# Expert layer on one core: forty-four finished activation tiles instead of thirty, gate chunks of sixteen tokens, gate builds placed between products

## The chip, the cores and the metric

One core of one Trainium2 chip. The metric is the device time of one execution in microseconds (us), here the median of three runs. PE is the matrix engine, PEld its weight load, DVE the vector engine, ACT the scalar engine, POOL GpSimd, SP the engine that issues most DMAs (SPq its queue).

## What is computed

512 tokens of width 1024 pass two transformer blocks. The change touches only the expert layer ("PEER") of the first. Each token picks 128 of 16384 experts (8 heads, 16 each); an expert is a row of `peer_u` and a row of `peer_v`:

```
u = peer_u[ix]                                   # 128 rows of 1024 for each token
a = gelu(einsum('td,thkd->thk', hx, u))
out = einsum('thk,thkd->td', gates * a, peer_v[ix])
```

The kernel computes this densely for the first 384 tokens (all 16384 activations, times a gate matrix that is zero where an expert was not picked) and by gathered rows for the last 128 tokens.

## The kernel before

All large products are float32 split into a high and a low part: `split` (L96, L97) writes `whi` on ACT and `wlo` on DVE or POOL, and three matmuls take the place of one. Weights come in loads of 1 MB (`wraw`, two buffers), each split in two halves (`whi`, `wlo`, four buffers).

The expert layer, `peer`, runs in this order:

1. **Heads.** Eight times: query product, scores, top-k on DVE (`head`), and between them a *group*: `u_group(g)` multiplies 256 experts with 384 tokens (48 matmuls of 384 columns, tile `lin`, lines L126 to L128) and ACT applies Gelu into two activation tiles `ga` (L521). Groups 0 to 6 lie here, 7 to 9 behind the last head. Then ACT takes the Exp of the gate scores `gt` (L657), DVE normalizes.
2. **Preparation and builds.** `prep` transposes expert numbers and gates (`ps_tr`, `tr`). Then 96 *builds* (`g_build`), each for four tokens: DVE makes two one-hot tiles `o1`, `o2` (L700, L701, six buffers each), POOL multiplies one by the gates (L702), PE multiplies them (`ps_g`, L704, four matmuls in the program, eight instructions in the trace), ACT copies the result into a staging tile `stg` (L706). Every 32 tokens (eight builds) the 2 MB of `stg` are written to DRAM (`gd`; the last chunk is `gl`, in three pieces). Groups 10 to 14 lie among the builds. Fifteen groups are thirty finished tiles `ga`, the 2 * U1 of the code.
3. **Tiles.** 128 times `v_tile(e)`: load 128 experts of `peer_v`, split them, multiply `ga` by the gates of four tiles' fetch `gq` (DVE, L792), split that into `gah` (ACT) and `gal` (DVE, L97), and 18 matmuls of 512 columns into six accumulators (`acc`, L801). The first of them needs `gah`, the fifth `gal`. From tile 21 on every second tile is followed by one more group (15 to 63), whose tiles go to a ring of RING = 10 buffers.
4. **Gathers** for the last 128 tokens run beside the tiles: POOL issues a gather of 128 rows (L740, 256 in all), DVE takes it with a dot product (L753) or a scaled add (L751). Four row buffers, eight from tile 30 on. A gather issued behind tile e waits for the end of tile e - 2 (PACE = 2). One is taken for each of the first 20 tiles, then nine for each four tiles.

Each engine works through a list of its own in order, and what stands behind a waiting instruction of its list waits too. A scheduler makes the lists from the order of the code and its own estimate of when things are ready.

## Time and profile before

| | |
|---|---|
| median of 3 runs | 2979.46 us (2977.13 to 2981.54) |
| the profiled execution | 2983.46 us, span of the trace 2981.7 us |
| busy share PE / PEld / DVE / ACT / POOL | 96% / 82% / 67% / 41% / 24% |
| chain that ended last, by engine | PE 72%, DVE 11%, DMA 7%, issue 5%, ACT 3%, POOL 2% |
| from the last head's scores to the last tile | 383.5 to 1548.3 us of the span |

Matmuls are pipelined, so that a PE shown as busy is not always one that does a new matmul as soon as it could. What a stretch could take at best is therefore read from the distance at which equal blocks of matmuls follow each other, and not from busy time.

### The profile page before, as it was taken

Reading aid. Unit: us, or ns where it says so; the run is one execution under the profiler, and the core shown is the slowest. Engines: PE = TensorE matmul, PEld = TensorE weight load, DVE = VectorE, ACT = ScalarE, POOL = GpSimd, SP = SyncE. Lnnn points to the kernel's source line nnn. Section 1 sums busy time; section 2 is a strip of 40 time slices with the busy share of each in tenths; the row PEclk is TensorE's granted clock in tenths of the full one; section 3 lists DMA queues with packets and bytes.
Section 4 is the critical chain, followed back from the end, with each engine's and each line's share of the span. In section 5 each row is a group of like instructions: output and inputs, shape, how many; then the busy total and the mean of one; then the engine's idle time right before and its main releaser. Section 6 shows DMA issues by size and latency. Waiting matters only on the chain.

```text
span 2981.7 us, 39362 instructions
## 1 busy us (share of the span) xinstructions
PE 2865.8 (96%) x14925; PEld 2442.2 (82%) x14925; DVE 1994.3 (67%) x3922; ACT 1220.4 (41%) x2017; POOL 724.0 (24%) x551
## 2 busy tenths in 40 slices
PE   7989988699999999999999999999999999999998
PEld 5778988678999998999976767888878888878886
DVE  7879988777877767787775455444557766654453
ACT  6543347633333333333344344223345555433223
POOL 0013458525554554455410000000021100100000
PEclk9999999899999999999999999999999999999999
DMA  7552234687987888788752222222221111122221
GB/s 258 181 198 86 86 113 199 253 282 280 353 312 280 287 297 293 277 297 295 290 178 77 71 71 76 94 99 99 99 75 55 44 42 36 50 99 99 99 99 57
DMA packets 133022, 487.19 MB, mean 163 GB/s; under 512 B 10593, under 2 KB 60129, under 8 KB 96610
## 3 DMA queue, kind: packets, MB, share of 16 engines
q1 hardware_dynamic: 95104, 349.33, 33.3%
q0 software_dynamic: 36864, 134.23, 12.1%
q8 instruction: 117, 1.92, 0.3%
q10 hardware_dynamic: 866, 1.13, 0.1%
q14 instruction: 71, 0.58, 0.1%
HBM read 455.29 MB, written 29.36 MB: 163 GB/s over the span
## 4 chain that ended last, share of the span: by engine, by line
PE 72%; DVE 11%; DMA 7%; issue 5%; ACT 3%; POOL 2%; SPq 0%; POOLq 0%; DVEq 0%; ACTq 0%
PE lin L126 15%; PE lin L127 15%; PE lin L128 15%; PE acc L801 10%; DMA rows<-peer_v,Ei 3%; PE ps_g L704 2%; DMA rows<-peer_u,Ei 1%; DVE wlo L97 1%; PE ps_x L1295 1%; PE psc L948 1%; PE ps_y L1301 1%; PE po L971 1%; POOL wlo L97 1%; PE in L260 1%; ACT whi L96 1%
## 5 line engine op out<-in xcount | busy, mean ns | idle before, releaser
L96 ACT ACTIVATE whi<-wraw 128x1024 fp32r<-128x1024 f32 (+2 forms) x500 | 522.1, 1045 | 1046.2 <-PE lin L127 678.0
L126 PE MATMUL lin<-xah,whi 128*128 128x512 f32 (+1 forms) x2112 | 782.8, 371 | 18.4 <-ACT ga L521 10.0
L128 PE MATMUL lin<-xah,wlo 128*128 128x512 f32 (+1 forms) x2112 | 777.9, 368 | 2.6 <-POOL wlo L97 2.6
L127 PE MATMUL lin<-xal,whi 128*128 128x512 f32 (+1 forms) x2112 | 778.5, 369 | 0.0
L97 DVE TENSOR_TENSOR wlo<-wraw,whi 128x1024 fp32r<-128x1024 f32 (+2 forms) x388 | 477.2, 1231 | 185.9 <-ACT whi L96 179.3
L97 POOL TENSOR_TENSOR wlo<-wraw,whi 128x1024 fp32r<-128x1024 f32 x112 | 289.7, 2600 | 834.8 <-ACT whi L96 660.8
L126 PEld LDWEIGHTS lin<-xah,whi 128*128 128x128 f32 x2112 | 399.1, 189 | 69.5 <-ACT ga L521 10.6
L128 PEld LDWEIGHTS lin<-xah,wlo 128*128 128x128 f32 x2112 | 399.2, 189 | 45.6 <-POOL wlo L97 3.0
L127 PEld LDWEIGHTS lin<-xal,whi 128*128 128x128 f32 x2112 | 399.3, 189 | 43.6 <-issue 2.4
L753 DVE CUSTOM_DVE_ANT_0 rows<-rows,hrow 128x1024 f32<-128x1024 f32 x128 | 184.2, 1439 | 118.6 <-DMA rows<-peer_u,Ei 118.5
L801 PE MATMUL acc<-whi,gah 128*128 128x512 f32 x768 | 239.6, 393 | 22.9 <-ACT gah L96 22.9
L751 DVE SCALAR_TENSOR_TENSOR gacc<-rows,acol,gacc 128x1024 f32<-128x1024 f32 x128 | 191.2, 1494 | 92.1 <-DMA rows<-peer_v,Ei 91.7
L801 PE MATMUL acc<-whi,gal 128*128 128x512 f32 x768 | 239.3, 393 | 7.5 <-DVE gal L97 7.5
L801 PE MATMUL acc<-wlo,gah 128*128 128x512 f32 x768 | 239.4, 393 | 4.0 <-DVE wlo L97 4.0
L740 POOL DMA_INDIRECT rows<-peer_u,Ei x128 | 156.0, 1218 | 202.3 <-PE acc L801 146.1
L127 PE MATMUL lin<-hl,whi 128*128 128x512 f32 x512 | 200.1, 391 | 0.0
L126 PE MATMUL lin<-hh,whi 128*128 128x512 f32 x512 | 199.3, 389 | 0.0
L128 PE MATMUL lin<-hh,wlo 128*128 128x512 f32 x512 | 199.2, 389 | 0.0
L740 POOL DMA_INDIRECT rows<-peer_v,Ei x128 | 157.5, 1230 | 166.6 <-PE acc L801 132.0
L801 PEld LDWEIGHTS acc<-whi,gah 128*128 128x128 f32 x768 | 144.5, 189 | 50.4 <-ACT gah L96 23.1
L801 PEld LDWEIGHTS acc<-whi,gal 128*128 128x128 f32 x768 | 144.9, 189 | 40.2 <-DVE gal L97 9.5
L801 PEld LDWEIGHTS acc<-wlo,gah 128*128 128x128 f32 x768 | 145.1, 189 | 37.2 <-DVE wlo L97 6.2
(460 smaller groups left out, 4163.3 us busy)
## 6 DMA issues: line engine op xcount, KB each, us to landing
wraw<-peer_ut SPq DMA_DIRECT2D x64, 1024.0 KB
wraw<-peer_v SPq DMA_DIRECT2D x64, 1024.0 KB
wraw<-w_up SPq DMA_DIRECT2D x32, 1024.0 KB
wraw<-w_down SPq DMA_DIRECT2D x32, 1024.0 KB
gd<-stg SPq DMA_DIRECT2D x11, 2048.0 KB
gq<-gd SPq DMA_DIRECT2D x32, 704.0 KB
ada_w<-w_ada SPq DMA_DIRECT2D x20, 1024.0 KB
wraw<-dn_w_in SPq DMA_DIRECT2D x16, 1024.0 KB
```

Source lines behind the costliest of these rows:

```text
L96: self.nc.scalar.activation(hi, x, AF.Copy)
L97: ins = (eng or self.nc.vector).tensor_tensor(lo, x, hi.bitcast(F32), op=ALU.subtract)
L126: nc.tensor.matmul(ps[:, :n], hi[:, i], xh[:, k, :n], start=(i == 0), stop=False)
L127: nc.tensor.matmul(ps[:, :n], hi[:, i], xl[:, k, :n], start=False, stop=False)
L128: nc.tensor.matmul(ps[:, :n], lo[:, i], xh[:, k, :n], start=False, stop=(k == ks[1] - 1))
L260: nc.tensor.matmul(acc[f], w[:, f * P:(f + 1) * P], v[:, k, :], start=(k == 0 and n == 0), stop=(k == NK - 1 and n == 2))
L704: nc.tensor.matmul(ps[:, t, :], o1[:, t, :], o2[:, t, :], start=True, stop=True)
L740: dma = nc.gpsimd.indirect_dma_start(out=rows[n], out_offset=None, in_=io[src], in_offset=bass.IndirectOffsetOnAxis(ap=Ei[:, j:j + 1], axi ...
L751: nc.vector.scalar_tensor_tensor(gacc, t, w, gacc, op0=ALU.mult, op1=ALU.add)
L753: nc.vector.tensor_tensor_reduce(t, t, hrow, 1.0, 0.0, op0=ALU.mult, op1=ALU.add, accum_out=w)
L801: mm = nc.tensor.matmul(acc[t][d], w[:, ts], r[:, d * T:(d + 1) * T], start=(e == 0 and f == 0), stop=(e == P - 1 and f == 2))
L948: nc.tensor.matmul(psc[u][:, :w], qT[us, j, qs], kT[us, j, :w], start=True, stop=True)
```

## The change

- `U1` 15 to 14, `RING` 10 to 16: 28 tiles in the first pool, 16 in the ring, which is now opened ahead of the builds. `last = (28 + 16) / 2 = 22` groups are finished ahead of the first tile, 44 tiles.
- Group 10 moves ahead of the preparation, and the Exp waits for the Gelu of group 9 (`held`).
- `GQ` 32 to 16: a chunk is four builds, 1 MB; 24 chunks. `GE = 8`: one fetch `gq` serves eight tiles (1.5 MB) in place of four (0.75 MB); runs of 512 bytes as before.
- `tick`: in groups 11 to 18, six builds are placed between the eight steps of each product. Groups 12 and 16 split on DVE, the others of them on POOL.
- `gate`: the first matmul of group 11 stands behind the preparation's transposes, and groups 19 to 21 behind the last build.
- Row buffers: `ROWS` 3 in place of 4, `MORE` 6 in place of 4: three, then nine from tile 28 on. Gathers taken: one for each of tiles 0 to 27, five for each two tiles from 28 to 111, one to tile 120, then two.
- The groups between tiles are 22 to 63, after tiles 29, 31, ..., 111.

```
-U1 = 15
-RING = 10
-MORE = 4
+U1 = 14
+RING = 16
+ROWS = 3
+MORE = 6
...
-                    nc.tensor.matmul(ps[:, :n], hi[:, i], xh[:, k, :n], start=(i == 0), stop=False)
+                    mm = nc.tensor.matmul(ps[:, :n], hi[:, i], xh[:, k, :n], start=(i == 0), stop=False)
+                    if self.gate is not None:
+                        self.after(mm, self.gate)
+                        self.gate = None
...
+                    if self.tick is not None:
+                        self.tick(k)
...
-                for g in range(7, 10):
+                for g in range(7, 11):
                     u_group(g, nc.gpsimd)
+                    if g == 9:
+                        held = box["gelu"]
...
-                nc.scalar.activation(g3, g3, AF.Exp)
+                self.after(nc.scalar.activation(g3, g3, AF.Exp), held)
...
-            GQ = 32
+            GQ = 16
+            GE = 8
...
+            ah.append(st.enter_context(tc.tile_pool(name="p_ah1", bufs=RING)))
...
-                            nc.tensor.transpose(ps[:, t, :], src[:, t, :], self.ident)
+                            self.gate = nc.tensor.transpose(ps[:, t, :], src[:, t, :], self.ident)
...
-                for g in range(10, U1):
-                    u_group(g, nc.gpsimd)
-                    pull(len(todo) if g > 12 else 32)
+                last = (2 * U1 + RING) // 2
+                self.tick = lambda k: pull(k % 4 != 2)
+                for g in range(11, last - 3):
+                    u_group(g, (nc.gpsimd, None)[g % 4 == 0])
+                self.tick = None
                 pull(len(todo))
+                self.gate = box["g"]
+                for g in range(last - 3, last):
+                    u_group(g)
...
-                    i = n % (4 + MORE) if len(pools) > 1 else n % 4
-                    pool, bufs = (sp, 4) if i < 4 else (pools[1], MORE)
+                    i = n % (ROWS + MORE) if len(pools) > 1 else n % ROWS
+                    pool, bufs = (sp, ROWS) if i < ROWS else (pools[1], MORE)
...
-                    if e % 4 == 0:
-                        g = sp.tile([P, NQ, 4, GQ], F32, tag="gq", name="gq")
-                        nc.sync.dma_start(out=g[:, :NQ - 1], in_=gd[:, :, e:e + 4, :].rearrange("q p e t -> p q e t"))
+                    if e % GE == 0:
+                        g = sp.tile([P, NQ, GE, GQ], F32, tag="gq", name="gq")
+                        nc.sync.dma_start(out=g[:, :NQ - 1], in_=gd[:, :, e:e + GE, :].rearrange("q p e t -> p q e t"))
...
-                    gather(1 if e < 2 * RING else 2 + (e % 4 == 0))
+                    gather(2 + (e % 2 == 0) if 2 * U1 <= e < P - RING else 1 + (e > P - 8))
                     n = e + RING
-                    if n >= 2 * U1 and n % 2 == 1 and n < P:
+                    if n >= 2 * U1 + RING and n % 2 == 1 and n < P:
                         u_group(n // 2, (None, nc.gpsimd)[n // 2 % 2])
```

Three places show how the lists move (names with numbers are buffers; the two kernels' lines differ by a few).

ACT behind the last head's scores; `ga` is a Gelu, `gt` the Exp. Before:

```order
L96 ACTIVATE whi_3804<-wraw_3802 128x1024
L521 ACTIVATE ga_3705<-lin_3680 128x384
L96 ACTIVATE whi_3835<-wraw_3802 128x1024
L521 ACTIVATE ga_3736<-lin_3711 128x384
L657 ACT_TABLE_LOAD
L657 ACTIVATE gt_1865<-gt_1865 128x512
L521 ACT_TABLE_LOAD
L521 ACTIVATE ga_3769<-lin_3744 128x384
```

The same place now (the Gelus `ga_3769` to `ga_3833` lie ahead of these rows):

```order
L99 ACTIVATE whi_3963<-wraw_3930 128x1024
L531 ACTIVATE ga_3864<-lin_3839 128x384
L99 ACTIVATE whi_4042<-wraw_4040 128x1024
L531 ACTIVATE ga_3897<-lin_3872 128x384
L99 ACTIVATE whi_4142<-wraw_4040 128x1024
L531 ACTIVATE ga_3928<-lin_3903 128x384
L669 ACT_TABLE_LOAD
L669 ACTIVATE gt_1865<-gt_1865 128x512
L99 ACTIVATE whi_4244<-wraw_4242 128x1024
L531 ACT_TABLE_LOAD
L531 ACTIVATE ga_3961<-lin_3936 128x384
```

The Exp stood ahead of the Gelus of groups 7 to 9 (`ga_3769` to `ga_3928`) and stands behind them now.

PE in the middle of the builds; each `ps_g` row is one build. Before:

```order
L704 MATMUL ps_g<-o_4196,o_4195 128x128 x4
L126 MATMUL lin<-xah,whi 128x384
L127 MATMUL lin<-xal,whi 128x384
L704 MATMUL ps_g<-o_4207,o_4206 128x128 x4
L128 MATMUL lin<-xah,wlo 128x384
L126 MATMUL lin<-xah,whi 128x384
L704 MATMUL ps_g<-o_4220,o_4219 128x128 x4
```

Now, in the same stretch:

```order
L716 MATMUL ps_g<-o_4213,o_4212 128x128 x4
L129 MATMUL lin<-xah,whi 128x384
L133 MATMUL lin<-xal,whi 128x384
L134 MATMUL lin<-xah,wlo 128x384
L129 MATMUL lin<-xah,whi 128x384
L133 MATMUL lin<-xal,whi 128x384
L134 MATMUL lin<-xah,wlo 128x384
L716 MATMUL ps_g<-o_4230,o_4229 128x128 x4
L129 MATMUL lin<-xah,whi 128x384
L133 MATMUL lin<-xal,whi 128x384
L134 MATMUL lin<-xah,wlo 128x384
L716 MATMUL ps_g<-o_4255,o_4254 128x128 x4
```

Two or three matmuls of a group stood between two builds; three or six do now, four on average.

ACT around the last build (`stg` copies builds, `gah` belongs to the first tile). Before:

```order
L706 ACTIVATE stg_5155<-ps_g_5222 128x4x128
L706 ACTIVATE stg_5155<-ps_g_5233 128x4x128
L96 ACTIVATE gah_5406<-ga_2307 128x384
L96 ACTIVATE gah_5442<-ga_2338 128x384
L96 ACTIVATE gah_5474<-ga_2540 128x384
```

Now:

```order
L718 ACTIVATE stg_5596<-ps_g_5642 128x4x128
L99 ACTIVATE whi_5788<-wraw_5786 128x1024
L531 ACTIVATE ga_5689<-lin_5664 128x384
L99 ACTIVATE whi_5819<-wraw_5786 128x1024
L531 ACTIVATE ga_5720<-lin_5695 128x384
L99 ACTIVATE whi_5873<-wraw_5871 128x1024
L531 ACTIVATE ga_5753<-lin_5728 128x384
L99 ACTIVATE gah_5878<-ga_2307 128x384
L99 ACTIVATE gah_5912<-ga_2338 128x384
L99 ACTIVATE whi_5907<-wraw_5871 128x1024
L531 ACTIVATE ga_5784<-lin_5759 128x384
```

The first `gah` followed the last copy at once; now three Gelus of the held groups lie between (19 twice, then the first of 20), and the second Gelu of group 20 (`ga_5784`) lies behind the first two `gah`.

## Rows read from the trace of the kernel before

**Rows 1.** Windows by stage: length, busy (count) of five engines, PE clock, DMA share, GB/s.
```profile
383.50:438.30 54.80, 44.80 (x249) 44.12 (x248) 41.78 (x139) 18.47 (x27) 27.30 (x14) 0.91 0.29 96
438.30:571.00 132.70, 122.76 (x961) 120.94 (x960) 116.81 (x184) 108.97 (x113) 106.88 (x98) 0.99 0.49 199
571.00:594.00 23.00, 0.06 (x2) 0.04 (x1) 5.13 (x9) 2.58 (x5) 4.88 (x5) 0.56 0.91 319
594.00:694.00 100.00, 94.29 (x396) 76.50 (x397) 73.49 (x112) 32.46 (x45) 26.59 (x25) 0.96 0.83 281
694.00:1502.00 808.00, 803.96 (x4081) 732.67 (x4080) 614.00 (x678) 282.37 (x395) 416.93 (x274) 1.00 0.82 296
1502.00:1548.30 46.30, 43.08 (x182) 34.80 (x180) 29.71 (x32) 16.14 (x23) 5.00 (x4) 0.96 0.55 197
```

**Rows 2.** Chain that ended last: start, length, what; two blocks of two tiles.
```profile
702.51 8.20 PE acc L801 x36
719.05 8.20 PE acc L801 x36
```

**Rows 3.** Waits of PE, whole span: us in total, times, longest.
```profile
PE acc L801 <- ACT gah L96: 22.9, 1, 22.9
PE lin L126 <- ACT ga L521: 10.0, 2, 8.9
PE ps_g L704 <- POOL o L702: 9.9, 5, 2.4
PE acc L801 <- DVE wlo L97: 4.0, 5, 1.1
```

**Rows 4.** Timeline behind the last head: start, length, engine, what, [idle before <-releaser].
```profile
406.31 0.63 ACT L657 ACTIVATE gt<-gt 128x512 f32<-128x512 f32 x1 [12.09 <-DVE gt L636]
408.79 0.69 PE L126 MATMUL lin<-xah,whi 128*128 128x384 f32 x1 [8.91 <-ACT ga L521]
```

**Rows 5.** Groups of lines, 450 to 565 us (busy, mean ns, idle before); then POOL's timeline.
```profile
L706 ACT ACTIVATE stg<-ps_g 128x512 f32<-128x512 f32 x80 | 86.2, 1094 | 23.2 <-PE ps_g L704 17.2 <-issue 2.8
L702 POOL TENSOR_TENSOR o<-o,tr 128x512 f32<-128x512 f32 x82 | 83.6, 1045 | 9.1 <-DVE o L701 5.9 <-PE ps_g L704 2.6 <-PE lin L128 0.6
L97 POOL TENSOR_TENSOR wlo<-wraw,whi 128x1024 fp32r<-128x1024 f32 x4 | 9.5, 2377 | 13.3 <-ACT whi L96 13.3
...
443.33 14.08 POOL L702 TENSOR_TENSOR o<-o,tr 128x512 f32<-128x512 f32 x14
```

**Rows 6.** Timeline from the last builds to the first tile, five engines.
```profile
566.39 4.63 PE L704 MATMUL ps_g<-o,o 128*128 128x128 f32 x40
572.99 1.29 SPq L712 DMA_DIRECT2D gl<-stg  x3
581.43 1.13 POOL L740 DMA_INDIRECT rows<-peer_u,Ei  x1 [13.29 <-DMA gl<-stg]
589.74 1.23 DVE L753 CUSTOM_DVE_ANT_0 rows<-rows,hrow 128x1024 f32<-128x1024 f32 x1 [7.97 <-DMA rows<-peer_u,Ei]
592.67 1.49 DVE L792 TENSOR_TENSOR ga<-ga,gq 128x384 f32<-128x384 f32 x3
593.38 0.94 ACT L96 ACTIVATE gah<-ga 128x384 fp32r<-128x384 f32 x2 [20.42 <-DVE ga L792]
```

**Rows 7.** Timeline of two gathers: issue on POOL, take on DVE, and a fetch between.
```profile
600.34 1.01 POOL L740 DMA_INDIRECT rows<-peer_u,Ei  x1 [8.16 <-PE acc L801]
605.50 1.22 DVE L753 CUSTOM_DVE_ANT_0 rows<-rows,hrow 128x1024 f32<-128x1024 f32 x1 [1.48 <-DMA rows<-peer_u,Ei]
608.50 1.11 POOL L740 DMA_INDIRECT rows<-peer_u,Ei  x1 [3.14 <-DVE wlo L97]
608.83 0.37 SPq L783 DMA_DIRECT2D gq<-gd  x1
618.97 1.23 DVE L753 CUSTOM_DVE_ANT_0 rows<-rows,hrow 128x1024 f32<-128x1024 f32 x1 [5.54 <-DMA rows<-peer_u,Ei]
```

**Rows 8.** Timeline of PE among the last ten tiles.
```profile
1521.38 0.73 PE L801 MATMUL acc<-whi,gal 128*128 128x512 f32 x2 [1.79 <-DVE gal L97]
```

More of the change, by code (lines that the diff above doesn't have):

```diff
@@ L516, in peer @@
             xd = dram.tile([P, NK, T], F32, name="xd")
+            box = {}
             def u_group(g, eng=None):
@@ L520, in gelu @@
                     A[e] = ah[e >= 2 * U1].tile([P, NG], F32, tag="ga", name="ga")
-                    nc.scalar.activation(A[e], ps[:, :NG], AF.Gelu)
+                    box["gelu"] = nc.scalar.activation(A[e], ps[:, :NG], AF.Gelu)
                 self.linear(io["peer_ut"], xh, xl, gelu, chunks=[g], n=NG, eng=eng)
@@ L703, in g_build @@
                     for t in range(4):
-                        nc.tensor.matmul(ps[:, t, :], o1[:, t, :], o2[:, t, :], start=True, stop=True)
+                        box["g"] = nc.tensor.matmul(ps[:, t, :], o1[:, t, :], o2[:, t, :], start=True, stop=True)
                     q = t0 % GQ
@@ L727, in peer @@
                        for t in range(3)]
-                rows = {-1: sp.tile([P, D], F32, tag="rows", bufs=4, name="rows")}
+                rows = {-1: sp.tile([P, D], F32, tag="rows", bufs=ROWS, name="rows")}
                 gacc = sp.tile([P, D], F32, bufs=1, name="gacc")
@@ L780, in v_tile @@
                 def v_tile(e):
-                    if e % 4 == 0:
-                        g = sp.tile([P, NQ, 4, GQ], F32, tag="gq", name="gq")
-                        nc.sync.dma_start(out=g[:, :NQ - 1], in_=gd[:, :, e:e + 4, :].rearrange("q p e t -> p q e t"))
+                    if e % GE == 0:
+                        g = sp.tile([P, NQ, GE, GQ], F32, tag="gq", name="gq")
+                        nc.sync.dma_start(out=g[:, :NQ - 1], in_=gd[:, :, e:e + GE, :].rearrange("q p e t -> p q e t"))
                         a, b, last = [v for v in gl if v[0] <= e < v[1]][0]
-                        nc.sync.dma_start(out=g[:, NQ - 1], in_=last[:, e - a:e - a + 4, :])
+                        nc.sync.dma_start(out=g[:, NQ - 1], in_=last[:, e - a:e - a + GE, :])
                         gq["g"] = g
@@ L824, in peer @@
                 for t in (2, 1, 0):
-                    o = sp.tile([P, D], F32, tag="rows", bufs=4, name="orow")
+                    o = sp.tile([P, D], F32, tag="rows", bufs=ROWS, name="orow")
                     for d in range(2):
```

8 lines of the change are left out of this document (4 added, 4 removed).

## The prediction, made before the change was run

> **What bounds the kernel now.** First the stages from the last head's scores to the last tile [rows 1]: 1164.8 us in which PE is shown busy nearly all the time except between the builds and the first tile. Busy time doesn't tell what PE could do at best, so the second view is the chain that ended last [rows 2]: two blocks of 36 tile matmuls begin 16.54 us apart, one lasts 8.20 us, and the 48 matmuls of a group fill the other 8.34 us. So a tile matmul costs 0.228 us (a tile of 18: 4.10 us) and a group matmul 0.174 us. Forty build instructions in a row take 4.63 us [rows 6], 0.116 us each, 0.93 us for a build of eight. With these prices the bare work of each stage, and what it loses, are:
>
> - Stage 1, 383.5 to 438.3: 237 group matmuls (45 of group 6, groups 7 to 9 and the first behind the preparation) 41.2 us, nine transposes at 0.116 us 1.0 us. Lost: 12.6 us.
> - Stage 2, to 571.0: 192 group matmuls 33.4 us, 96 builds 88.9 us. Lost: 10.4 us.
> - Stage 3, to 594.0: no work at all. Lost: 23.0 us.
> - Stage 4, to 694.0: 22 tiles, 90.2 us. Lost: 9.8 us.
> - Stage 5, to 1502.0: 49 groups and 96 tiles, 802.4 us. Lost: 5.6 us.
> - Stage 6, to 1548.3: 10 tiles, 41.0 us. Lost: 5.3 us.
>
> PE is the bound, and 66.7 us are lost on it. Third, PE's own waits [rows 3] say to whom: one wait of 22.9 us for the first `gah`, 10.0 us for Gelus, 9.9 us for POOL's part of the builds, 4.0 us for weight splits among the tiles. The rest is mostly the clock: its mean is 0.91, 0.96 and 0.96 in stages 1, 4 and 6 [rows 1], so 8% of stage 4, 8 us, ran at 1.2 in place of 2.4 GHz and lost 4 us, after PE had stood still.
>
> The change neither adds nor removes a matmul: groups 15 to 21 move from between the tiles to a place ahead of them. So the sum is: which of the lost microseconds go, and which come.
>
> **The Exp (stage 1).** Before, the Exp stood ahead of the Gelus of group 7 and waited 12.09 us for DVE's last scores, until 406.31; PE, whose two product buffers were full, waited 8.91 us until 408.79 [rows 4] and then ran slow. Now the Gelus of groups 7 to 9 come first. PE ends group 9 at 383.5 + 189 x 0.174 = 416.3, ten us behind the time at which the Exp's input is ready, and group 10, 8.3 us, runs on PE while ACT and DVE finish the gates. All 12.6 us go. What is late next is the first build: its transposes are followed by copies on ACT, two compares on DVE and a multiplication on POOL, for which 48 matmuls were cover and now only 18 are, 3.1 us. I put 1 us of waiting there (bounds 0 and 3), counted in stage 2.
>
> **The builds (stage 2).** The work is now 384 group matmuls, 66.7 us, and the same 88.9 us: 155.6 us. POOL's 9.9 us of waits came as four of up to 2.4 us and one short one, the length of one POOL split (2.377 us) put between its multiplications [rows 3, 5]. POOL needs 14.08 / 14 = 1.0 us for each multiplication [rows 5], against 1.38 us at which PE came for the builds (stage 2 divided by 96), so it regained little. Now PE comes every 155.6 / 96 = 1.62 us. In the 9.7 us of one product with its six builds, POOL has 6 x 1.0 + 2.4 = 8.4 us of work; ACT has six copies of 1.09 us and about 1.5 us for split and Gelu (an estimate from the mean of 1.05 us on the page), 8.1 us. PE stays the bound, and six buffers take up one split, once POOL has run ahead. The first of the twelve POOL splits stands behind four multiplications and finds no lead. I take 3 us for the first ones (bounds 0, and 28.5 us if all twelve cost what each did before). Lost now: 4 us in place of 10.4.
>
> Staging is new: a chunk is 1 MB and its buffer is wanted again two chunks later. Two chunks are 13.0 us of builds, the copies of one reach over 3 x 1.62 + 1.09 = 5.9 us, so a write may take 7.0 us without cost. The nearest row is the last write of 2 MB: from its issue at 572.99 to the first instruction that waited for it, 581.43, 8.4 us [rows 6]. Half the bytes take between 4.2 and 8.4 us; I take 5, nearer to the half, since the row also holds an issue in three pieces, and so nothing. At 8.4 us each of some 22 chunks would wait half the excess, 0.7 us: 15 us. The Trainium skill, page "SBUF — State Buffer", section on the DMA setup-cost knee, speaks against this edit: each transfer pays about 2 us whatever its size, so one should move as much as possible in one. By its figure the twelve added writes cost 24 us if nothing covers them, and one write of 1 MB takes 4.4 us (an estimate from that page); with the first the time would be 2964 us, with the second the sum stays.
>
> **The held groups (stage 3).** The chain that PE waited for runs [rows 6]: last build 571.0, write issued 573.0, landed and first gather issued 581.4, first take 589.7, first `ga` 592.7, first `gah` 593.4. The cover is now three groups, 144 x 0.174 = 25.0 us. The chain loses about 3 us by the smaller last write (bounds 0 and 4.2) and gains the third gather, its take and a weight split, which stand ahead of the first `ga` on DVE: about 3.5 us, of a take's 1.23 us, a split of that order, and 1.1 us for one more issue on POOL. So the first `ga` comes some 22 us behind the last build, three before the cover ends. But the second Gelu of group 20 stands behind two `gah` (0.94 us) and a split on ACT, and the second product of group 21 needs that Gelu's buffer 20.9 us behind the last build. 22 + 2.4 gives 24.4: a wait of 3.5 us, 4 us with the clock (bounds 0, and 12 if the doubled fetch of 1.5 MB adds 8 us, which is what 581.4 to 589.7 took). The three groups themselves come out of stage 5. Lost: 4 in place of 23.0.
>
> **Tiles alone (stage 4).** The stretch grows from 22 to 30 tiles, 123.0 us bare. A gather is issued at the end of tile e - 2, and its take stands ahead of the `gal` of tile e + 1 in DVE's list, before (four buffers, take e + 3) as now (three buffers, take e + 2). So from the end of tile e - 2 there are two tiles and four matmuls, 9.1 us; less 0.4 us until POOL starts and 1.85 us for take and `gal`, 6.85 us from issue to take. One gather was ready after 5.2 us, another after 10.5 us, with a fetch issued 0.3 us behind it [rows 7]: that one held PE 3.4 us. DVE multiplies about three tiles' `ga` in each tile until all finished ones are done, so dense fetching lasts 16 tiles in place of 11. I scale: 9.8 us less 2 us for the slow start, which goes with stage 3's wait, are 7.8 us in 22 tiles, 10 us in 30 (bounds 4, and 34 if every gather takes 10.5 us).
>
> **Groups and tiles (stage 5).** 42 groups and 82 tiles, 686.5 us bare. Gathers are five a pair of tiles in place of four and a half: with two loads of 1.05 MB, a fetch's share of 0.39 MB and gathers of 0.52 MB each, 5.1 MB in 16.54 us, 309 GB/s where 296 are measured at a DMA share of 0.82 [rows 1]. And where six more row buffers open, at tile 28, DVE's list holds eight takes in a row. I take 8 us (bounds 4 and 20) in place of 5.6.
>
> **The last tiles (stage 6).** Sixteen alone in place of ten. Two takes a tile stood in the way of `gal` [rows 8]; now it is one, issued up to nine ahead. Lost: 1 (bounds 0 and 5.3) in place of 5.3.
>
> **Sum.** Lost now 0 + 4 + 4 + 10 + 8 + 1 = 27 us, in place of 66.7: 39.7 us less. From the profiled execution's 2983.5 us that gives 2943.8; the median of the runs lies 4.0 us below that execution, so 2940 us.
>
> **Rivals.** (a) POOL or staging binds the builds: twelve splits at 2.4 us, or 15 us for late writes and some splits. For it: POOL's reserve is 1.3 us in 9.7. Against: it regained nothing before only because PE came every 1.38 us. Stage 2 loses 28.5 us in place of 4: 2964 us. (b) Nearly all is hidden: lost 9 us (stages 4 and 5 at their lower ends, 1 elsewhere): 2922 us. For it: 48 pairs lost only 5.6 us. (c) Slower: the gathers bind the tiles alone. Three row buffers and a fetch twice as large make each of 28 gathers late. A gather that takes L costs (L - 6.85) / 3 us a tile, since three tiles lie in the loop. At 10.5 us, the slowest in the rows, this is 34 us, 2964 us and still faster. It eats the whole gain of 40 us from L = 12.2 us on; at 14 us it costs 67 us, and the time is 2997 us. For it: 1.5 MB at 309 GB/s are 4.9 us, twice the fetch of before. Against: fetches are issued for eight tiles, and most gathers lie beside none. The Trainium skill, page "DMA: Bandwidth & Descriptors", section "Queues, rings and completion order", says that each DMA engine goes round its queues packet by packet; a gather would then share with a fetch and not stand behind all of it, which keeps L near 10.5 us; by the order of issue it would be about 2.4 us more, 12.9 us, and the time 2986 us if every gather met a fetch. No row separates the two. (d) That the change doesn't do what it says: the lists show each of its moves, so I give it nothing.
>
> **How the numbers follow.** Forecast 0.70, (a) 0.11, (b) 0.11, (c) 0.05, no change 0.03. A difference under 0.2%, 6 us, can't be told from none here. Faster: the forecast nearly whole, (a) and (b), 0.91; same 0.04; slower 0.05. The range leaves out little more than (c) and the outer halves of (a) and (b): 2921 to 2966 us.
>
> **What would show it.** In the profile of the changed kernel: no wait of PE for a Gelu near 400 us; the waits for POOL's `o` under 5 us in all; at most some 5 us of wait around the first `gah`, and a clock that stays at 2.4 GHz there; 30 tiles in some 133 us; pairs at 16.54 us; no wait among the last ten tiles. The prediction is wrong if builds come later than every 1.7 us, if PE waits for `gal` in most of the tiles 2 to 27, or if a wait of over 12 us stands behind the held groups.

## The result, and the profile after

| | before | after |
|---|---|---|
| median | 2978.30 us (2975.51 to 2981.54, run beside it) | 2944.26 us (2941.28 to 2945.99) |
| profiled execution, span | 2983.46, 2981.7 us | 2945.99, 2944.0 us |

Each median is of four runs. The ratio is 0.9884, 95% interval 0.9867 to 0.9901: 34.0 us less, clearly outside the 0.2% that count as no change. The time lies 4 us above the forecast of 2940 us and inside its range.

The windows by stage answer to [rows 1]; the boundaries are the same events (first group matmul behind the last head, the point behind 237 group matmuls and the transposes, last build, first tile, first group among the tiles, last group, last tile).

```profile
378.70:421.00 42.30, 42.30 (x250) 42.27 (x249) 40.47 (x128) 18.80 (x26) 20.97 (x9) 1.00 0.36 125
421.00:580.00 159.00, 154.50 (x1154) 153.50 (x1152) 129.51 (x198) 121.07 (x131) 121.45 (x106) 0.99 0.53 206
580.00:614.50 34.50, 27.73 (x146) 27.41 (x145) 18.08 (x26) 9.54 (x15) 4.11 (x4) 0.85 0.87 285
614.50:753.40 138.90, 128.57 (x542) 102.14 (x541) 99.72 (x146) 46.26 (x62) 45.02 (x38) 0.98 0.87 301
753.40:1440.20 686.80, 686.80 (x3494) 627.53 (x3493) 550.23 (x613) 242.11 (x339) 398.67 (x249) 1.00 0.85 309
1440.20:1509.30 69.10, 66.12 (x290) 53.72 (x288) 41.27 (x46) 25.51 (x35) 11.06 (x8) 1.00 0.58 198
```

Stage 3, which held no matmul before, now holds 144; stage 5 shows PE busy throughout. With the prediction's own prices (group matmul 0.174, tile 4.10, build 0.93 us) the lost time of each stage is:

| stage | lost before | forecast | lost after |
|---|---|---|---|
| 1, Exp | 12.6 | 0 | 0 |
| 2, builds | 10.4 | 4 | 3.5 |
| 3, held groups | 23.0 | 4 | 9.6 |
| 4, 30 tiles alone | 9.8 (22 tiles) | 10 | 15.9 |
| 5, groups and tiles | 5.6 | 8 | 0 |
| 6, last tiles | 5.3 | 1 | 3.5 |
| sum | 66.7 | 27 | 32.5 |

Stage 6 ends in both windows 1.4 us behind its last tile matmul (1507.83 now, 1546.87 before), so that 1.4 us of its 3.5 and of its 5.3 are no waits among tiles.

So the stages gave 34.2 us of the span's 37.7. The rest is outside: stage 1 begins 4.8 us earlier (378.7 against 383.5), in code that the change does not touch, and what lies behind the last tile is 1.3 us longer. The start of stage 1 lay between 378.8 and 384.4 us in the experiments too, all with this same code ahead of it; it is a difference from run to run.

PE's waits over the whole span answer to [rows 3] (us in total, times, longest):

```profile
PE acc L817 <- DVE gal L100: 11.8, 11, 3.9
PE lin L129 <- ACT ga L531: 6.8, 1, 6.8
...
PE ps_g L716 <- POOL o L714: 4.5, 3, 2.3
```

The 22.9 us at the first `gah` are gone, and the 9.9 us behind POOL are 4.5. What is left is `gal`, in eleven pieces among the tiles, and one wait of 6.8 us inside the held groups.

### The profile page after: what moved, and what is told of

Read it like the earlier page. It is cut to its first block, busy times and chain, and to the rows that moved or that the text cites. A ratio compares the mean times of both kernels' runs of the same rounds, so it can differ in the third digit from the quotient of the medians.

```text
span 2944.0 us, 39329 instructions
## 1 busy us (share of the span) xinstructions
PE 2857.7 (97%) x14925; PEld 2435.8 (83%) x14925; DVE 1992.8 (68%) x3926; ACT 1222.7 (42%) x2017; POOL 738.2 (25%) x547
## 4 chain that ended last, share of the span: by engine, by line
PE 76%; DVE 10%; DMA 7%; issue 4%; ACT 2%; POOL 1%; POOLq 0%; SPq 0%; DVEq 0%; ACTq 0%
PE lin L129 16%; PE lin L133 16%; PE lin L134 16%; PE acc L817 12%; PE ps_g L716 3%; DMA rows<-peer_u,Ei 3%; PE ps_x L1311 1%; PE psc L964 1%; DMA wraw<-peer_ut 1%; PE ps_y L1317 1%; DVE wlo L100 1%; PE po L987 1%; DMA ada_w<-w_ada 1%; ACT whi L99 1%; PE pt L979 1%
## 5 line engine op out<-in xcount | busy, mean ns | idle before, releaser
L100 POOL TENSOR_TENSOR wlo<-wraw,whi 128x1024 fp32r<-128x1024 f32 x108 | 283.8, 2645 | 780.9 <-ACT whi L99 682.9
L756 POOL DMA_INDIRECT rows<-peer_v,Ei x128 | 169.9, 1327 | 223.2 <-PE acc L817 174.9
L767 DVE SCALAR_TENSOR_TENSOR gacc<-rows,acol,gacc 128x1024 f32<-128x1024 f32 x128 | 183.7, 1435 | 44.3 <-DMA rows<-peer_v,Ei 43.7
L756 POOL DMA_INDIRECT rows<-peer_u,Ei x128 | 163.8, 1280 | 132.4 <-PE acc L817 58.0
```

The lines of the kernel that those rows point to most:

```text
L100: ins = (eng or self.nc.vector).tensor_tensor(lo, x, hi.bitcast(F32), op=ALU.subtract)
L756: dma = nc.gpsimd.indirect_dma_start(out=rows[n], out_offset=None, in_=io[src], in_offset=bass.IndirectOffsetOnAxis(ap=Ei[:, j:j + 1], axi ...
L767: nc.vector.scalar_tensor_tensor(gacc, t, w, gacc, op0=ALU.mult, op1=ALU.add)
```

## Experiments

All start from the changed kernel. A stage's length is read from PE's first and last instruction of it, and the table carries every run's, so that an edit is judged in the stage in which it lies (us; stage 1 begins at the first group matmul behind the last head; stage 2 includes 1.1 us of transposes; stage 6 ends with the last tile matmul; tile 29 belongs to stage 4). The stages are those of one profiled execution of each kernel, which need not be the median one: that of e10_old_first lies 7.6 us above its median, that of e12_best 6.2 us above, that of e2_hold0 3.2 us below.

| kernel | median | 1 | 2 | 3 | 4 | 5 | 6 |
|---|---|---|---|---|---|---|---|
| changed kernel | 2944.3 | 41.2 | 160.3 | 34.3 | 138.9 | 686.9 | 67.5 |
| e1_exp_free | 2960.6 | 56.7 | 158.8 | 35.4 | 142.4 | 687.2 | 65.7 |
| e2_hold0 | 2955.0 | 41.2 | 178.4 | 21.6 | 141.5 | 687.2 | 66.7 |
| e3_pace3 | 2950.5 | 41.2 | 158.8 | 33.5 | 142.3 | 688.1 | 65.4 |
| e4_hold4 | 2946.4 | 41.2 | 155.1 | 39.0 | 137.3 | 687.7 | 65.7 |
| e5_take_late | 2943.2 | 41.2 | 160.4 | 34.8 | 139.1 | 686.9 | 66.1 |
| e6_gah_late | 2946.0 | 41.2 | 160.4 | 26.3 | 148.1 | 686.9 | 66.5 |
| e7_ramp | 2951.1 | 42.3 | 160.6 | 32.4 | 137.9 | 688.6 | 69.0 |
| e8_all | 2938.6 | 41.2 | 160.3 | 25.8 | 138.7 | 686.9 | 69.9 |
| e9_ga_paced | 2977.1 | 41.9 | 160.6 | 34.7 | 129.8 | 728.0 | 66.3 |
| e10_old_first | 2944.0 | 41.2 | 160.4 | 34.5 | 142.6 | 688.7 | 65.9 |
| e11_dve_split | 2946.9 | 41.2 | 158.8 | 33.3 | 139.2 | 687.3 | 65.9 |
| e12_best | 2930.6 | 41.2 | 154.3 | 25.3 | 141.0 | 688.8 | 68.5 |

Where an edit leaves a stage alone, its length still moves: stage 4 was 138.9, 142.4 and 141.5 us in three kernels that are the same there. Differences of under 4 us in stage 4 say nothing, and stage 2 took 158.8 us in e1 and e3, which leave it alone, too.

### The Exp

```
-                self.after(nc.scalar.activation(g3, g3, AF.Exp), held)
+                nc.scalar.activation(g3, g3, AF.Exp)
```

> The changed kernel without the one edge that holds the Exp behind the Gelu of group 9: ACT then has the Exp ahead of the Gelus of group 7, as before the change, and PE's order stays the same. Theory (every microsecond that PE stands still in stage 1 counts once): a wait of PE for a Gelu of about 9 us returns near 400 us, stage 1 loses about 12.6 us again, time 2944 + 12 = 2956 us (2953 to 2959). Rival (the wait was given back later, since the builds are bound by POOL or ACT, which run on meanwhile): stage 1 loses as much, stage 2 regains most of it, time 2944 to 2948 us.

The wait is back, longer than before (ACT's and PE's timeline of this run: start, length, engine, what, idle before and releaser):

```profile
404.96 0.63 ACT L669 ACTIVATE gt<-gt 128x512 f32<-128x512 f32 x1 [15.01 <-DVE gt L646]
407.44 0.69 PE L129 MATMUL lin<-xah,whi 128*128 128x384 f32 x1 [11.84 <-ACT ga L531]
```

Stage 1 took 15.5 us more. Stages 2 and 3 together took 194.2 us against 194.6, so nothing was given back, and the median is 16.3 us higher. The first theory holds in kind; stage 1 lost 15.5 us where it had 12.6, and the time lies 1.6 us above its range. In this one edge lies nearly half of the change's gain.

### Held groups: none, and four

None: groups 11 to 13 run ahead of the builds instead.

```
+                for g in range(11, 14):
+                    u_group(g)
-                for g in range(11, last - 3):
+                for g in range(14, last):
...
-                self.gate = box["g"]
-                for g in range(last - 3, last):
-                    u_group(g)
```

> The changed kernel with no group held: groups 11 to 13 run without builds ahead of group 14, and the builds lie in groups 14 to 21, so that the last build is followed by the first tile at once. Same work, same 30 tiles alone. Theory (the three held groups are 25.0 us of cover for a chain of about 25 us that does not depend on them): stage 3 loses 24 to 28 us in place of 9.6, the first builds wait no longer (2 us less in stage 2), time 2944 + 15 = 2959 us (2955 to 2963). Rival (the chain is long because the loads, splits and Gelus of the held groups stand in its way): without them the first ga comes 18 to 20 us behind the last build, stage 3 loses 20 us, time 2952 us or less.

In the traces stages 2 and 3 together took 200.0 us in place of 194.6: only 5.4 us more. Two things made it less than the theory's 15. PE waited 21.6 us in stage 3, not 24 to 28:

```profile
PE acc L816 <- ACT gah L99: 21.6, 1, 21.6
```

so the chain without held groups is shorter than with them, as the rival had it: the first `ga` came 20.3 us behind the last build, and 24.8 us in the changed kernel. And no wait for POOL is left in stage 2, since POOL and DVE work ahead during the three groups. Cover in front of the first build and cover behind the last one are the same three groups: the change spent them behind, for a net 5.4 us in these traces. By the medians it is 10.7 us, at the theory's lower bound. The five runs reach from 2949.5 to 2965.4 us, the profiled one took 2951.8, and what the two longest lost is in no trace.

Four:

```
-                self.tick = lambda k: pull(k % 4 != 2)
-                for g in range(11, last - 3):
+                self.tick = lambda k: pull(k != 6)
+                for g in range(11, last - 4):
...
-                for g in range(last - 3, last):
+                for g in range(last - 4, last):
```

> The changed kernel with four groups held and seven builds placed in each product of groups 11 to 17. Theory (stage 3's 9.6 us are a cover of 25.0 us too short for a chain of 24.8 us to the first ga and 27.7 us to the Gelu that PE waited for, and the low clock behind that wait): with 33.4 us of cover stage 3 loses 0 to 1 us; the builds stay hidden, POOL having 7 x 1.0 + 2.4 = 9.4 us of work in the 10.7 us of a product, so stage 2 loses 3 to 5 us; time 2944 - 8 = 2936 us (2934 to 2938). Rival (seven builds a product are too dense for POOL and ACT): stage 2 loses 10 us or more, time 2941 to 2950 us.

194.1 us for the two stages, against 194.6. The Gelu wait shrank from 6.8 to 2.5 us, and with seven builds a product POOL's waits grew from 4.5 to 6.9 us:

```profile
PE ps_g L716 <- POOL o L714: 6.9, 5, 2.3
PE lin L129 <- ACT ga L531: 2.5, 1, 2.5
```

The theory was half right about the cover, since stage 3 lost 5.6 us of its 39.0 where it had 0 to 1; and the rival's price for POOL, 10 us or more, did not come, though the denser builds cost about as much as the cover gave. More cover alone was not what stage 3 lacked, since a wait remained under 33.4 us of it.

### What stands in the lists of the held groups

DVE, ACT and PE around the held groups of the changed kernel, in order of time (same columns), answer to [rows 6]:

```profile
581.67 1.27 SPq L724 DMA_DIRECT2D gl<-stg  x3
587.72 1.13 POOL L756 DMA_INDIRECT rows<-peer_u,Ei  x1 [13.01 <-DMA gl<-stg]
596.62 1.23 DVE L769 CUSTOM_DVE_ANT_0 rows<-rows,hrow 128x1024 f32<-128x1024 f32 x1 [5.94 <-DMA rows<-peer_u,Ei]
602.45 1.23 DVE L769 CUSTOM_DVE_ANT_0 rows<-rows,hrow 128x1024 f32<-128x1024 f32 x1 [2.23 <-DMA rows<-peer_u,Ei]
603.60 1.22 DVE L100 TENSOR_TENSOR wlo<-wraw,whi 128x1024 fp32r<-128x1024 f32 x1
604.74 1.49 DVE L808 TENSOR_TENSOR ga<-ga,gq 128x384 f32<-128x384 f32 x3
605.45 0.94 ACT L99 ACTIVATE gah<-ga 128x384 fp32r<-128x384 f32 x2 [11.48 <-issue]
607.24 0.47 ACT L531 ACTIVATE ga<-lin 128x384 f32<-128x384 f32 x1
607.76 0.69 PE L129 MATMUL lin<-xah,whi 128*128 128x384 f32 x1 [6.77 <-ACT ga L531]
```

The first take comes 16.7 us behind the last build, 18.7 us before. But the third take is at 602.45: its gather landed 11.5 us after its issue. Behind it stand a weight split and the first `ga` on DVE, behind these ACT's `gah`, at which ACT stood for 11.48 us, and behind that, in ACT's list, the Gelu that PE needs. One edit frees ACT:

```
+                    if e == 0:
+                        self.after(self.hi_ins, gelus[-2])
```

(`hi_ins` is the `gah` of tile 0, `gelus[-2]` the Gelu of group 21's first product.)

> The changed kernel with the first gah held behind the Gelu of the first product of the last held group, so that ACT no longer stands at it with splits and Gelus of the held groups behind it. Theory (stage 3's loss is an order of lists: ACT waits 11.5 us at gah, DVE's last wlo stands behind three takes): the Gelu wait of 6.8 us goes, the wlo at 603.6 us, 3.5 us late, becomes the next wait, stage 3 loses 3 to 5 us in place of 9.6, time 2944 - 5 = 2939 us. Rival (cover too short for the chain as a whole, fetch and first ga): the first tile then waits itself for gah, stage 3 loses 7 us or more, time 2942 us or more.

Stage 3 fell to 26.3 us, and the wait moved one step on, to `gal` of the first tile:

```profile
610.64 0.73 PE L821 MATMUL acc<-whi,gah 128*128 128x512 f32 x2 [1.38 <-ACT gah L99]
617.12 1.22 PE L821 MATMUL acc<-whi,gal 128*128 128x512 f32 x2 [5.29 <-DVE gal L100]
```

DVE, still behind the third take, did eight `ga` and a fourth take before that `gal`. ACT's order was a cause, but not the only list in the wrong order; neither expectation was met, and stages 3 and 4 together took 174.4 us against 173.2. In e8_all (below) the takes of tiles 1 and 2 stand behind the first `gal`, too: stage 3 is 25.8 us, and tiles 0 to 3 lose 0.8 us in all. With both lists in order three groups are cover enough.

### The tiles alone

Stage 4 is the stage whose loss grew. Three theories were tried on it. First, more room for a gather:

```
-PACE = 2
+PACE = 3
```

> The changed kernel with PACE 3 in place of 2: a gather may start one tile earlier, when its buffer is free, so that from issue to take there are about 10.7 us in place of 6.85. Theory (the tiles alone lose their time in the loop of issue, landing and take, at landings of 4 to 9 us): the waits of tiles 4 to 19 (about 9 us of stage 4's 15.9) go, stage 4 loses 6 to 8 us (tile 29 with its burst of gathers stays), time 2944 - 8 = 2936 us (2934 to 2939). Rival (the DMA engines are the limit in the tiles alone: what starts earlier lands as much later): stage 4 within 2 us of 15.9, time 2942 to 2946 us.

No gain. But the edit didn't make the room: the scheduler moved the takes one tile ahead as well. Gather 10 (POOL) and its take (DVE), first of the changed kernel, then of this run:

```profile
645.22 1.17 POOL L756 DMA_INDIRECT rows<-peer_u,Ei  x1 [2.98 <-DVE acol L769]
654.24 1.22 DVE L769 CUSTOM_DVE_ANT_0 rows<-rows,hrow 128x1024 f32<-128x1024 f32 x1
```

```profile
638.94 1.21 POOL L756 DMA_INDIRECT rows<-peer_u,Ei  x1 [3.00 <-DVE acol L769]
647.46 1.23 DVE L769 CUSTOM_DVE_ANT_0 rows<-rows,hrow 128x1024 f32<-128x1024 f32 x1 [1.42 <-DMA rows<-peer_u,Ei]
```

9.0 us from issue to take, and 8.5. The run says nothing about its rival. So the takes were moved instead, gathers staying where they were (`late` goes around both instructions of a take, `gals` holds the `gal` so far):

```
+                def late(ins):
+                    if 3 < len(gals) <= 2 * U1:
+                        self.after(ins, gals[-2])
```

> The changed kernel with each take of the tiles 3 to 27 put behind the gal of the tile before it, one place later in DVE's list; gathers are issued as before (PACE 2). From issue to take there are then about 10.9 us in place of 6.85. Theory (late gathers make the losses of tiles 4 to 19): the landings of 7 to 9 us no longer reach PE, tiles 3 to 27 lose 2 to 4 us in place of about 9, stage 4 as a whole 9 to 11 us, time 2944 - 7 = 2937 us (2934 to 2940). Rival (DVE is full there: take 1.15, gal 0.47, wlo 1.14, three ga 1.41 are 4.16 us a tile, more than a tile's 4.08 on PE, so a wait for rows is passed on wherever the take stands): tiles 3 to 27 lose 7 us or more, time 2942 to 2946 us.

No gain again, and this time the list shows why. DVE's waits, tiles 1 to 28:

```profile
DVE rows L774 <- DMA rows<-peer_u,Ei: 16.3, 6, 4.8
DVE ga L814 <- DMA gq<-gl: 8.1, 3, 3.8
```

In the changed kernel the second wait is 0.8 us. With the takes out of the way DVE ran on to `ga` of tiles that come 8, 23 and 28 tiles later, and stood there for their fetch with `gal` of the next tile behind it. The rival is nearer: in tiles 4 to 12 of the changed kernel DVE is full between its waits for rows (busy 27.7 of 30 us from 631 to 661). Two takes in its timeline there:

```profile
639.73 1.22 DVE L769 CUSTOM_DVE_ANT_0 rows<-rows,hrow 128x1024 f32<-128x1024 f32 x1
640.87 0.55 DVE L100 TENSOR_TENSOR gal<-ga,gah 128x384 fp32r<-128x384 f32 x1
641.34 1.22 DVE L100 TENSOR_TENSOR wlo<-wraw,whi 128x1024 fp32r<-128x1024 f32 x1
642.48 1.49 DVE L808 TENSOR_TENSOR ga<-ga,gq 128x384 f32<-128x384 f32 x3
643.88 1.22 DVE L769 CUSTOM_DVE_ANT_0 rows<-rows,hrow 128x1024 f32<-128x1024 f32 x1
```

From take to take 4.15 us without a gap, where a tile takes PE 4.08. So DVE can make up nothing, and what it waits for is handed on to PE. The next run adds to the one above that each `ga` (`mul`) stands behind the `gal` of four tiles before:

```
+                    if len(gals) >= 4:
+                        self.after(mul, gals[-4])
```

> The run with the takes of tiles 3 to 27 one place later, and besides the multiplication of each ga by its gates held behind the gal of four tiles before, so that DVE does one a tile in place of three and does not stand at a fetch that only tile e + 8 needs. Theory (DVE's list is the cause: first it was full, 4.16 us a tile, then it waited 8.1 us for fetches with gal queued behind): with 3.2 us of DVE work a tile, gathers with 10.9 us and fetches far ahead of use, tiles 0 to 28 lose 0 to 3 us in place of about 9; tile 29 stays; time 2944 - 7 = 2937 us (2935 to 2940). Rival (the DMA engines carry too much in this stretch, 1.25 MB a tile): weight loads come late instead, tiles 0 to 28 lose 6 us or more, time 2941 us or more.

The theory misses the sum by 40 us, and the rival has the time but not its loss in the stage. The stage answers: tiles 0 to 28 lose about 2 us in place of 9, stage 4 is the shortest of all runs, and PE's only wait in these tiles is

```profile
PE acc L825 <- DVE gal L100: 1.6, 1, 1.6
```

The order of DVE's list, with gathers given more room, was the cause of that loss. The edit also thins the fetches (the DMA engines' share of the first 47 us falls from 0.96 to 0.75), but gathers landed no sooner for it: after 4.0 to 9.2 us, 6.1 on average, where the changed kernel has 4.0 to 8.9 and 6.2. The pacing without the late takes was not run. The price came in stage 5, 41 us. SP's and ACT's timeline at its start, and PE's waits for Gelus in the whole stage:

```profile
745.57 13.70 SPq L107 DMA_DIRECT2D wraw<-peer_ut  x1
769.76 1.06 ACT L99 ACTIVATE whi<-wraw 128x1024 fp32r<-128x1024 f32 x1 [21.03 <-DMA wraw<-peer_ut]
PE lin L130 <- ACT ga L532: 23.0, 8, 7.1
```

The later `ga` free the fetch buffers later. In SP's list the sixth and the seventh fetch then stand between the first loads of `peer_ut`, all of which the changed kernel has behind the seventh; the issue of one load took 13.70 us in place of 0.33, and its split waited 21 us. The same order comes back every eight tiles, a load of `peer_ut` right behind the fetch, with up to 6.4 us for its issue, and PE's eight waits lie over the whole stage. In the changed kernel the small last piece of a fetch, `gl`, stands there, its issue takes 10.3 to 13.2 us, and in the whole of stage 5 PE waits for nothing:

```profile
788.41 10.31 SPq L801 DMA_DIRECT2D gq<-gl  x1
```

A fetch blocks what stands behind it on SP, and that costs where it is a load that is needed soon.

### Tile 29

Of stage 4's 15.9 us, 6.8 belong to one tile: 10.9 us in place of 4.1. SP, POOL, DVE and PE in the changed kernel:

```profile
735.07 0.33 SPq L836 DMA_DIRECT2D x<-xd  x1
735.80 1.18 POOL L756 DMA_INDIRECT rows<-peer_u,Ei  x1 [3.81 <-issue]
745.69 1.23 DVE L769 CUSTOM_DVE_ANT_0 rows<-rows,hrow 128x1024 f32<-128x1024 f32 x1 [6.67 <-DMA rows<-peer_u,Ei]
747.45 1.22 PE L817 MATMUL acc<-whi,gal 128*128 128x512 f32 x2 [3.90 <-DVE gal L100]
```

Gather 30, the first into a new buffer, is followed by eight more within 11 us and lands 9.2 us after its issue. Two edits on it, buffers opened one by one, and old buffers first:

```
-                        depth = ROWS + MORE if len(pools) > 1 else ROWS
+                        depth = ROWS + min(MORE, max(0, len(done) - 2 * U1))
...
-                    gather(2 + (e % 2 == 0) if 2 * U1 <= e < P - RING else 1 + (e > P - 8))
+                    gather(2 + (e % 2 == 0 and e > 2 * U1 + 5) if 2 * U1 <= e < P - RING else 1 + (e > P - 8))
```

> The changed kernel with the six added row buffers opened one for each tile from tile 28 on, in place of all at once, and two takes for each of tiles 28 to 33. Theory (sixteen gathers issued in a row land 9 to 12 us after their issue and hold gal of tile 29): the wait of 3.9 us there and the low clock behind it go, tile 29 takes 4.1 to 5.5 us in place of 10.9, time 2944 - 6 = 2938 us. Rival (tile 29 waits for DVE's or ACT's work at the change of the loop, not for gathers): tile 29 loses 5 us or more, time 2943 to 2946 us.

```
-                    i = n % (ROWS + MORE) if len(pools) > 1 else n % ROWS
+                    i = (n - 2 * U1 - ROWS + 1) % (ROWS + MORE) if len(pools) > 1 else n % ROWS
```

> The changed kernel with the order of the row buffers turned at tile 28: gathers 30 to 32 go to the three old buffers, 33 to 38 to the six new ones. Theory (gather 30 was issued at 735.8 us, some 4 us later than one a tile, since the new buffers lie where the last of the 28 ga were read, and then landed in 9.2 us beside nine others): gather 30 is issued near 732 us, lands in 5 to 7 us, and tile 29 takes 4.1 to 5.5 us in place of 10.9; time 2944 - 6 = 2938 us (2936 to 2941). Rival (the burst makes it late wherever its buffer is): gather 30 lands 8 us or more after its issue, tile 29 takes 7 us or more, time 2941 us or more.

By tile 29 both rivals won, and neither for the reason it gave: it took 10.2 us and 11.3 us. (The time of e7, 2951.1 us, lies above its rival's too; its stages, 1.7 us more than the changed kernel's in all, don't say why, and the intervals of the two ratios overlap.) In e10 gather 30 was issued on time, 4.1 us behind gather 29, and landed after 10.0 us; in e7 after 9.4 us. In e12_best (below) only one other gather was issued in the 7 us behind it, and it still took 9.4 us. So neither lateness nor a burst is needed. What stands ahead of gather 30 in all of them, by 0.7 to 1.4 us, is the first row of the fence above: the load of `x`, 2 MB, which the program has behind tile 96 and the scheduler puts where its space comes free, at tile 28. Over tile 28 and 29 the DMA engines are full (length, five engines' busy time, clock, DMA share, GB/s; the two windows behind the first tile are for comparison):

```profile
614.50:661.50 47.00, 44.07 (x192) 35.05 (x191) 38.73 (x64) 16.62 (x22) 10.86 (x10) 1.00 0.96 316
661.50:735.00 73.50, 70.08 (x302) 55.75 (x300) 50.04 (x70) 25.90 (x35) 20.75 (x16) 1.00 0.79 272
735.00:753.40 18.40, 14.43 (x51) 11.34 (x51) 10.95 (x15) 3.73 (x6) 13.41 (x12) 0.81 0.95 377
```

Before, the same load was issued at 751.3 us, among pairs, and PE did not wait near it. In e3_pace3 gather 30 came ahead of the load. POOL's issue of gather 30, the load, the issue of gather 31, and the two takes:

```profile
730.62 0.93 POOL L756 DMA_INDIRECT rows<-peer_u,Ei  x1 [3.03 <-PE acc L817]
733.31 0.33 SPq L836 DMA_DIRECT2D x<-xd  x1
733.56 1.67 POOL L756 DMA_INDIRECT rows<-peer_u,Ei  x1 [2.00 <-DVE gal L100]
735.83 1.23 DVE L769 CUSTOM_DVE_ANT_0 rows<-rows,hrow 128x1024 f32<-128x1024 f32 x1 [1.41 <-DMA rows<-peer_u,Ei]
745.74 1.23 DVE L769 CUSTOM_DVE_ANT_0 rows<-rows,hrow 128x1024 f32<-128x1024 f32 x1 [8.20 <-DMA rows<-peer_u,Ei]
```

Gather 30 landed there after 4.8 us, and gather 31, right behind the load, after 10.4 us: late is the first gather behind the `x` load, whichever it is. What moving the load would give back is open; a kernel that moves it was not tried.

### Splits among the builds

```
-                    u_group(g, (nc.gpsimd, None)[g % 4 == 0])
+                    u_group(g, (nc.gpsimd, None)[g in (11, 12, 14, 16, 18)])
```

> The changed kernel with the weight splits of groups 11, 12, 14, 16 and 18 on DVE (before: 12 and 16), so that POOL's first splits come when it has run ahead. Theory (stage 2's loss is POOL's: 4.5 us of waits behind splits of 2.38 us, 3.4 us at 1.2 GHz behind one of them): the waits fall under 1.5 us, stage 2 takes 156 to 158 us in place of 160.3, time 2944 - 3 = 2941 us. Rival (DVE, busy 130 of 160 us, comes late with the compares instead): PE waits for POOL's o or DVE's o as long as before, stage 2 takes 160 us or more.

PE waited 4.5 us for POOL as before, in the same three places, and stage 2 took 158.8 us, between theory and rival. The edit missed: splits run two groups ahead, so that those of group 11 lie ahead of the builds, and the first two between POOL's multiplications are group 13's. In e12_best group 13 went to DVE: the waits fell to 0.5 us, stage 2 to 154.3 us.

### The edits together

e8_all joins the takes one place later (from tile 1 on), `gah` behind the Gelu, and the opening one by one.

> The three edits together: takes of tiles 1 to 27 one place later (so that in the held groups only the first take stands ahead of DVE's last wlo), the first gah behind the Gelu of the last held group's first product, row buffers opened one by one. Theory (the three losses are separate and each is an order of lists): stage 3 loses 0 to 2 us, stage 4 4 to 6 us, together 20 us less than the changed kernel's 25.5, time 2944 - 20 = 2924 us (2921 to 2929). Rival (the DMA engines are the limit: what no longer waits in one place waits in the next): stages 4 and 5 together lose 12 us or more, time 2932 us or more.

2938.6 us. Stage 3 came as the theory had it. Stage 4 didn't shrink: tile 4 took 10.5 us (DVE at `ga`, 3.4 us for a fetch, as in e5) and tile 29 stayed. Stages 4 and 5 lost 15.7 us together, so the rival's numbers are met: what no longer waited in one place waited in the next. Its reason, that the DMA engines are the limit, is not shown by this run.

e12_best has the first two edits of e8_all, the split of group 13, and these:

```
+                    if 3 <= e < 2 * U1 + RING:
+                        self.after(mul, gals[3 * e // 5 - 1])
...
-                        depth = ROWS + MORE if len(pools) > 1 else ROWS
+                        depth = ROWS + min(MORE, max(0, len(done) - 2 * U1 - 2))
...
-                    gather(2 + (e % 2 == 0) if 2 * U1 <= e < P - RING else 1 + (e > P - 8))
+                    gather(2 + (e % 2 == 0) if 2 * U1 + 2 <= e < P - RING else 1 + (e > P - 8))
```

> The changed kernel with five edits of order, each read from the runs before: takes of tiles 1 to 27 behind the gal of the tile before; the first gah behind the Gelu of the last held group's first product; the multiplication of ga spread over the tiles (five ga in three tiles, up to the last of the 44); the added row buffers opened one a tile from tile 30, with one take for each of tiles 28 and 29; the split of group 13 on DVE with those of 12 and 16. Theory (the changed kernel's losses in stages 2 to 4 are orders of lists, and the burst of gathers at tile 28 is the fifth): stage 2 157 to 160 us in place of 160.3, stage 3 25 to 27 in place of 34.3, stage 4 124 to 128 in place of 138.9, stage 5 687 to 690, time 2944 - 21 = 2923 us (2919 to 2929). Rival (spread fetches and later gathers collide with the loads of stage 5, as in the run with ga held four tiles): stage 5 takes 695 us or more, time 2931 us or more.

2930.58 us (2926.99 to 2936.79), ratio to before 0.9828 (0.9814 to 0.9842), against 0.9884 (0.9867 to 0.9901) of the changed kernel: it beats both. Neither theory nor rival is met whole. Stages 2 and 3 gave 15 us, stage 2 more than expected. PE waits 0.3 us for the first `gah` there, and

```profile
PE ps_g L719 <- POOL o L717: 0.5, 1, 0.5
```

Stage 4 gave nothing in the trace: tiles 0 to 11 lose 0.3 us, but later ones wait, and tile 29 with them. With the fetches spread, weight loads stand behind them on SP and come late. The longest issue of such a load, and ACT's waits for loads from 600 to 722 us (8.2 us in four pieces over the same tiles of the changed kernel):

```profile
658.94 5.03 SPq L107 DMA_DIRECT2D wraw<-peer_v  x1
ACT whi L99 <- DMA wraw<-peer_v: 31.8, 9, 7.7
```

A rate between this one and that of e9, or fetches on another queue, is the open lead.

## Why the prediction was right, and which terms were not

The stages were to give 39.7 us and gave 34.2. Part of this closeness is luck: the held groups, the tiles alone and the last tiles lost 14.0 us more than forecast, the builds and the groups with tiles 8.5 us less. And 4.8 us of the profiled gain come from the earlier start of stage 1, which no term foresaw.

- **The Exp: right.** All 12.6 us went, nothing came back (e1), and the price of the lost edge is 15.5 us.
- **The builds: right in sum, by two errors.** Forecast 4, measured 3.5 by the prices used. But e12_best ran the same work in 154.3 us where those prices, with transposes, make 156.7: 0.93 us for a build was read from forty build instructions in a row [rows 6]. Two builds of the changed kernel with six group matmuls between them:

```profile
577.20 1.05 PE L716 MATMUL ps_g<-o,o 128*128 128x128 f32 x8
579.13 1.05 PE L716 MATMUL ps_g<-o,o 128*128 128x128 f32 x8
```

  They begin 1.93 us apart, of which the six matmuls are 1.04: a build costs 0.89 us here, and the stage lost about 7 us. By e12_best it is 6.5: 4.5 us behind POOL, and most of the rest is 3.4 us at 1.2 GHz behind one of these waits, which cost 1.7. The waits stood where the step put them, at the first build and at POOL's first splits, 0.5, 2.3 and 1.7 us. Twelve splits did not cost; rival (a) fell.
- **Staging: right.** PE never waited for a write. The last one of 1 MB took 5.4 us, from 581.67 to the instruction that waited for it, 587.04; I had taken 5, and bounds of 4.2 and 8.4. The page of the Trainium skill, "SBUF — State Buffer", section on the DMA setup-cost knee, gave 4.4 us for it, an estimate from that page and 1 us below the trace. Its first reading, a price for each added write, did not come.
- **The held groups: mechanism right, size wrong.** Forecast 4, measured 9.6. The first `ga` came 24.8 us behind the last build in place of 22. The smaller write was to save 3 us, and the first take came 2.0 us sooner. The larger step that failed is the third gather, "about 3.5 us" for take, split and issue, with the landing left out: it landed 11.5 us after its issue, where the first two took 7.5 and 7.6, and from the first take to the first `ga` it was 8.1 us, 5.2 more than before. So the wait was 6.8 us in place of 3.5. The clock behind it, put at half a microsecond, cost 2.7: PE ran at 1.2 GHz for another 5.4 us. The Gelu that PE waited for is the one that the step names; e6_gah_late and e8_all show that its place in ACT's list, and the third take's in DVE's, are what cost.
- **Tiles alone: right in kind, wrong in cause and place.** Forecast 10, measured 15.9; but 6.8 of that is tile 29, which the forecast had counted as a burst among the 8 us of stage 5, where 0 was lost. The two together: 18 forecast, 15.9 measured. For the 9.1 us of tiles 0 to 28 the loop of a gather was the right frame (landings up to 8.9 us against room for 6.85), but "DVE multiplies about three tiles' `ga` in each tile" should have been priced: it makes 4.15 us of DVE work a tile, above PE's 4.08.
- **Groups and tiles: wrong.** Forecast 8, bounds 4 and 20; measured 0. The load on the DMA engines came as the sum had it, 309 GB/s at a share of 0.85, but its price did not: in this stage PE waited for nothing. The loss at the new row buffers came one tile earlier, in tile 29, which is stage 4's.
- **The last tiles:** 3.5 in place of 1, but 1.4 of it lies behind the last tile matmul, which the forecast of 1 left out; of the rest two waits for `gal` are 0.74 and 0.80 us.
- **The signs.** As forecast: no wait for a Gelu near 400 us, 4.5 us in all behind POOL, builds every 1.66 us. Not so: the clock in the held groups (a mean of 0.85 in stage 3), the 30 tiles (138.9 us, not 133), and no wait among the last tiles.
- **Rivals.** (b) fell with stages 3 and 4. (c) came only as far as landings of 4.0 to 8.9 us in tiles 4 to 28, under the 12.2 us from which it decides. Four of these gathers were issued 1.0 to 2.2 us behind a fetch, and landed after 7.2 to 8.9 us. The first packet of each moved 4.0 to 5.7 us after its issue. One was issued from 623.16 to 624.10 us; from 624.2 to 628.1 us all packets on the DMA engines were of SP's queue, q1 (packets, MB, share; gathers are on q0):

```profile
q1 hardware_dynamic: 2241, 1.15, 104.0%
```

  The rule that the prediction cited, "DMA: Bandwidth & Descriptors", section "Queues, rings and completion order" of the Trainium skill, has each DMA engine go round its queues packet by packet. The trace does not agree with it for these first microseconds, in which a gather got no share beside a fetch; later in its landing packets of both move. Nor did one of these gathers come to the 12.9 us of the other order. On SP's own queue loads did stand behind fetches (e9, e12).

## What to carry to other kernels

Cover that is measured in microseconds of matmuls only counts if nothing that the covering work needs stands behind the covered wait in an engine's list: look for the waiting instruction, then at what is queued behind it. Work that a scheduler does early because it can (multiplications up to 28 tiles ahead, a load when its space comes free) fills an engine or the DMA queues at the moment when little else hides it. Judge an edit in its own stage first, and check in the order that it did what it was meant to: two of twelve here didn't.
